# Combining three dilated attention groups: weights per token and head instead of per element, and two slots more for a split operand

## The chip, the cores and the metric

The kernel runs on one core of a Trainium2 chip. The metric is the device time of one execution in microseconds (us). TensorE does the matrix products, VectorE (DVE) and ScalarE (ACT) the elementwise work, GpSimd (POOL) and SyncE (SP) mostly issue transfers; 16 DMA engines move the data.

## The reference

One layer of an encoder over 1024 tokens with 1024 features, all in float32. Three branches of token mixing read the same normalized input: dilated attention (A), retention (R) and attention into a memory (M). Each is projected, gated and added:

```
merged = gate_A*(y_A @ W_pa) + gate_R*(y_R @ W_pr) + gate_M*(y_M @ W_pm)
h = h + merged @ W_out
```

Branch A has three groups of 4 heads of 64, with dilations 1, 4 and 16 (a group with dilation d works on d interleaved subsequences). The change is in how the groups are weighted: a softmax over the groups' log-sum-exp, per token and head.

```
alpha = softmax(stack([lse_0, lse_1, lse_2]), axis=0)     # per head, token
y_A   = stack([o_0, o_1, o_2]) * alpha[..., None]
```

## The kernel before

**Products.** A float32 product is made of three matmuls on rounded operands: each operand is split into a high and a low part (`hilo`: a cast on ScalarE makes `wh` or `yh`, a subtraction on VectorE makes `wl` or `yl`), and `mm3` issues high x high, high x low and low x high. The weights stream from DRAM through SyncE's queue into `wraw` and are split on arrival.

**Dilated attention.** Six pairs of heads, numbered i = 0 to 5 as 3s + g (g the group, s the half of its 4 heads). `attn_dil(i)` loads q, k and v of the pair (`qkv_d`, issued by SyncE), computes scores, and leaves in `U` (128 rows: 2 heads x 64 features; 1024 tokens) the output, stored to `u_d`; and per token and head the negated maximum `nm` and the sum `l`, on 128x16 tiles. Inside a dilated pair the tokens stand in the order of the subsequences; `unperm` puts U back into token order when it leaves PSUM. This stage is merged with the twelve steps of the gates, whose weights are the `wraw<-in_w_gate_dram` of SyncE's queue; TensorE has its matmuls to do there while the pairs' scores go through the other engines.

**Projections.** Then come three projections, one for each branch, in the order R, M, A (`s0`, `s1`, `s2`; b0, b1, b2 are the branches). `proj_steps` does 8 blocks of 128 output features each; a block accumulates over kt = 6, 4 and 6 slabs of y, in PSUM tiles `accg`: 36, 24 and 36 matmuls. The slabs are loaded raw (`yraw`, by SyncE) and split into `yh` and `yl`, which live in a pool of 12 slots (6 slabs): a slab of the next branch gets a slot when the last block of the one before has read its last. `yraw`, `U` and the gates `sg` share a pool of 8 slots of their own (`ab`).

**Combining.** `combine(s)` weighs the three groups of half s, and stores to `ya_d`, from which the third projection reads. Both calls are merged with the first projection. It computes lse = ln(l) - nm on 128x16 tiles; `spread` repeats each value over 64 columns (`lw`), TensorE transposes `lw` into PSUM (`pst`), and ScalarE copies it, put into token order, to a full tile `L` of 128x1024. Then `comb` works on halves of 128x512: maximum, three subtractions, three exponentials, sum, reciprocal, and two multiplications of U per group.

**Order.** The program is written in steps which a scheduler merges into one fixed order for each engine; an engine waits at its next instruction until its inputs and its slot are there. A DMA that waits holds up those behind it on the queue of the same engine.

Of the kernel before, what the change touches and what calls it, by code (L numbers as in the profile page):

```python
# [17 lines left out]
P = 128  # L18
# [130 lines left out]
def encoder_block(ctx: ExitStack, tc: tile.TileContext, x, mem, vec, w_mix, w_gate, w_pa, w_pr, w_pm,  # L149
# [26 lines left out]
    u_d = dram.tile([6 * P, S], F32, name="u_d")  # L176
    sg_d = dram.tile([3 * D, S], F32, name="sg_d")
# [602 lines left out]
    def attn_dil(i, ap_, stats):  # L780
# [7 lines left out]
        def begin():  # L788
            for j, n in ((2, "v"), (0, "q"), (1, "k")):
                st[n] = ab(n)  # L790
                nc.sync.dma_start(st[n], qkv_d[(3 * i + j) * P:(3 * i + j + 1) * P, :])
            loc["V"] = ap_.tile([P, 11, P], F32, name="V", tag="V")
            loc["U"] = ap_.tile([P, S], F32, name="U", tag="U")
            loc["nm"] = st_p.tile([P, 2, 8], F32, name="nm", tag="nm", bufs=6)
            loc["l"] = st_p.tile([P, 2, 8], F32, name="l", tag="l", bufs=6)
# [72 lines left out]
        def tail():  # L868
            stats[i] = (loc["nm"], loc["l"])
            nc.gpsimd.dma_start(u_d[i * P:(i + 1) * P, :], loc["U"])  # L870

# [17 lines left out]

    def combine(s, stats, ap_):  # L890
        loc = {}

        def lse():
            loc["st"] = [stats[3 * s + g] for g in range(3)]
            loc["U"] = [ab("U") for g in range(3)]
            for g in range(3):
                nc.gpsimd.dma_start(loc["U"][g], u_d[(3 * s + g) * P:(3 * s + g + 1) * P, :])
            loc["lse"] = ap_.tile([P, 3, 2, 8], F32, name="lse", tag="lse")
            for g in range(3):
                nc.vector.tensor_copy(loc["lse"][:, g], loc["st"][g][1])  # L900
            nc.scalar.activation(loc["lse"], loc["lse"], AF.Ln)
            for g in range(3):
                nc.vector.tensor_sub(loc["lse"][:, g], loc["lse"][:, g], loc["st"][g][0])
            loc["L"] = []

        def spread(g):
            loc["w"] = []
            for b in range(2):
                W2 = ap_.tile([P, 4, 2, 64], F32, name="lw", tag="sm", bufs=3)
                nc.vector.tensor_copy(W2, loc["lse"][:, g, :, 4 * b:4 * b + 4].rearrange("p h t -> p t h")  # L910
                                      [:, :, :, None].to_broadcast([P, 4, 2, 64]))
                loc["w"].append(W2)

        def bcast(g):
            L = ap_.tile([P, S], F32, name="L", tag="L", bufs=3)
            for b, W2 in enumerate(loc.pop("w")):
# [4 lines left out]
                if DIL[g] == 1:  # L921
                    nc.scalar.copy(L[:, b * HALF:(b + 1) * HALF], ps)
                else:
                    unperm(L, ps, DIL[g], b)
            loc["L"].append(L)

        def comb(h):
            c = slice(h * HALF, (h + 1) * HALF)
            L = [t[:, c] for t in loc["L"]]
            m = ap_.tile([P, HALF], F32, name="cm", tag="sm", bufs=3)  # L930
            z = ap_.tile([P, HALF], F32, name="cz", tag="sm", bufs=3)
            nc.vector.tensor_tensor(m, L[0], L[1], op=ALU.max)
            nc.vector.tensor_tensor(m, m, L[2], op=ALU.max)
            for g in range(3):
                nc.vector.tensor_sub(L[g], L[g], m)
                nc.scalar.activation(L[g], L[g], AF.Exp)
            nc.vector.tensor_add(z, L[0], L[1])
            nc.vector.tensor_add(z, z, L[2])
            for a in range(2):
                nc.vector.reciprocal(z[:, a * 256:(a + 1) * 256], z[:, a * 256:(a + 1) * 256])  # L940
            for g in range(3):
                u = loc["U"][g][:, c]
                k = 2 * g + s
                nc.vector.tensor_mul(u, u, L[g])
                nc.vector.tensor_mul(u, u, z)
                (nc.gpsimd, nc.scalar)[s].dma_start(ya_d[k * P:(k + 1) * P, c], u)

        steps = [lambda g=g, f=f: f(g) for g in range(3) for f in (spread, bcast)]
        return [lse] + steps + [lambda: comb(0), lambda: comb(1)]
# [147 lines left out]
    def y_part(r):  # L1097

        a, b = (y_p.tile([P, S], F32R, name=t, tag="y", bufs=12) for t in ("yh", "yl"))
        hilo(a, b, r)  # L1100
        return a, b
# [110 lines left out]
    def y_load(bi, ks):  # L1212
        for k in ks:
            y_r[bi, k] = y_raw(bi, k)
# [9 lines left out]
    def y_split(bi, kt):  # L1224
        y_load(bi, [k for k in range(kt) if (bi, k) not in y_r])
        y_hl[bi] = list(zip(*[y_part(y_r.pop((bi, k))) for k in range(kt)]))
# [7 lines left out]
    psb.update(pool=psG, bufs={"t": 2})  # L1234
    cb_p = pg.enter_context(pool("cb_p", side="right"))
# [3 lines left out]
    def proj_steps(bi, kt):  # L1239
        def begin():  # L1240
            if bi not in y_hl:
                y_split(bi, kt)
# [28 lines left out]
    run(merge(s0, combine(0, stats, cb_p) + combine(1, stats, cb_p)))  # L1271
    y_load(b1, range(2))
    run(s1[:-2])
# [499 lines left out]
```

## Time and profile before

| | |
|---|---|
| time, median of 3 runs | 1881.91 us (1880.28 to 1887.35) |
| profiled execution: its own time | 1879.56 us |
| its span, first to last instruction | 1877.8 us |
| busy in the span: TensorE, VectorE, ScalarE | 98%, 69%, 50% |

The times of single instructions come from the profiled execution, and count from the start of its span. 1.76 us of its time lie outside the span. A busy share is an average over stages of different kinds, so a stage is read by its own stretch of time.

### The profile page before, as it was taken

How to read it: one execution, taken by the hardware profiler on the slowest of the kernel's cores; microseconds unless marked ns; L12 is line 12 of the kernel's file. 1: busy time of each engine (PE TensorE's matmuls, PEld its weight loads, DVE VectorE, ACT ScalarE, POOL GpSimd, SP SyncE). 2: the span in 40 equal slices, each digit the busy share in tenths (PEclk: the TensorE clock that was granted, in tenths of full speed). 3: DMA queues.
4: the chain of work that ended last, by engine and by line, in shares of the span. 5: the costliest groups of instructions: out<-in, count | busy, mean ns of one | idle time of the engine just before them, and what ended most of it. 6: DMA issues, size and time to landing. Idle time of an engine off the chain costs nothing.

```text
span 1877.8 us, 24304 instructions
## 1 busy us (share of the span) xinstructions
PE 1831.2 (98%) x9254; PEld 1520.4 (81%) x9254; DVE 1290.9 (69%) x2243; ACT 930.9 (50%) x1524; POOL 120.4 (6%) x222
## 2 busy tenths in 40 slices
PE   7999999999999999999998999989999999999997
PEld 6889988888877777777786889967888888888886
DVE  7554464658796555555588654577888787899976
ACT  7354342435686566655633223545454545445444
POOL 1000010110000000000110100000000000020001
PEclk9999999999999999999998999989999999999999
DMA  6211112112233333224546625312232222296543
GB/s 254 90 51 51 46 34 68 68 60 87 79 118 118 113 124 112 77 92 166 192 157 218 210 88 204 104 43 90 68 101 79 90 79 90 91 353 247 176 161 118
DMA packets 65989, 223.70 MB, mean 119 GB/s; under 512 B 7760, under 2 KB 7888, under 8 KB 65744
## 3 DMA queue, kind: packets, MB, share of 16 engines
q1 hardware_dynamic: 41760, 138.77, 21.7%
q0 software_dynamic: 22096, 79.70, 11.2%
q10 hardware_dynamic: 2016, 3.67, 0.5%
q8 instruction: 73, 1.20, 0.3%
q14 instruction: 44, 0.36, 0.1%
HBM read 168.64 MB, written 53.48 MB: 118 GB/s over the span
## 4 chain that ended last, share of the span: by engine, by line
PE 86%; DVE 6%; ACT 5%; issue 2%; DMA 1%; POOL 0%; SPq 0%; POOLq 0%; ACTq 0%; DVEq 0%
PE ps L182 11%; PE ps L183 11%; PE ps L181 11%; PE acc L183 6%; PE acc L181 6%; PE acc L182 6%; PE w L181 5%; PE w L182 4%; PE w L183 4%; PE accg L182 2%; PE accg L183 2%; PE accg L181 2%; PE psu L859 2%; PE pss L815 2%; ACT sw L546 2%
## 5 line engine op out<-in xcount | busy, mean ns | idle before, releaser
L186 ACT CAST wh<-wraw 128x1024 fp32r<-128x1024 f32 (+2 forms) x273 | 261.8, 961 | 308.2 <-PE accg L182 84.4
L187 DVE TENSOR_TENSOR wl<-wraw,wh 128x1024 fp32r<-128x1024 f32 (+2 forms) x273 | 303.5, 1113 | 123.8 <-ACT wh L186 118.9
L181 PE MATMUL acc<-nTh,wh 128*128 128x512 f32 x384 | 152.3, 397 | 0.0
L183 PE MATMUL acc<-nTh,wl 128*128 128x512 f32 x384 | 150.4, 392 | 0.0
L182 PE MATMUL acc<-nTl,wh 128*128 128x512 f32 x384 | 150.1, 391 | 0.0
L181 PE MATMUL ps<-wh,th 128*128 128x512 f32 x308 | 119.8, 389 | 0.0
L182 PE MATMUL ps<-wl,th 128*128 128x512 f32 x308 | 119.8, 389 | 0.0
L183 PE MATMUL ps<-wh,th 128*128 128x512 f32 x308 | 119.8, 389 | 0.0
L181 PE MATMUL w<-nTh,wh 128*128 128x512 f32 x272 | 110.6, 407 | 0.0
L182 PE MATMUL accg<-yl,wh 128*128 128x512 f32 x256 | 101.7, 399 | 8.5 <-DVE yl L187 8.5
L182 PE MATMUL w<-nTl,wh 128*128 128x512 f32 x272 | 106.5, 391 | 0.0
L183 PE MATMUL w<-nTh,wl 128*128 128x512 f32 x272 | 106.4, 391 | 0.0
L181 PE MATMUL accg<-yh,wh 128*128 128x512 f32 x256 | 99.3, 397 | 1.7 <-ACT yh L186 1.7
L183 PE MATMUL accg<-yh,wl 128*128 128x512 f32 x256 | 100.7, 395 | 0.0
L183 PEld LDWEIGHTS acc<-nTh,wl 128*128 128x128 f32 x384 | 72.1, 188 | 14.3
L181 PEld LDWEIGHTS acc<-nTh,wh 128*128 128x128 f32 x384 | 72.2, 188 | 14.2 <-DVE rt L548 0.3
L182 PEld LDWEIGHTS acc<-nTl,wh 128*128 128x128 f32 x384 | 72.2, 188 | 13.4
L181 PE MATMUL pso<-wh,mg 128*128 128x256 f32 x256 | 73.2, 286 | 0.0
L186 ACT CAST th<-g 128x512 fp32r<-128x512 f32 x66 | 40.7, 620 | 64.6 <-PE ps L183 43.2
L183 PE MATMUL pso<-wh,mg 128*128 128x256 f32 x256 | 72.5, 283 | 0.0
L182 PE MATMUL pso<-wl,mg 128*128 128x256 f32 x256 | 72.5, 283 | 0.0
L181 PE MATMUL ps<-b,wh 128*128 128x512 f32 x176 | 68.7, 390 | 0.0
(398 smaller groups left out, 4759.3 us busy)
## 6 DMA issues: line engine op xcount, KB each, us to landing
wraw<-in_w_mlp_dram SPq DMA_DIRECT2D x90, 512.0 KB, 4.1
wraw<-in_w_mix_dram SPq DMA_DIRECT2D x48, 512.0 KB, 3.6
wraw<-in_w_gate_dram SPq DMA_DIRECT2D x24, 512.0 KB, 3.6
sg<-sg_d POOLq DMA_DIRECT2D x24, 512.0 KB, 6.0
g_d<-cv POOLq DMA_DIRECT2D x22, 512.0 KB, 2.9
g<-g_d POOLq DMA_DIRECT2D x22, 512.0 KB, 13.6
wraw<-in_w_out_dram SPq DMA_DIRECT2D x16, 512.0 KB, 3.8
sg_d<-ub POOLq DMA_DIRECT2D x12, 512.0 KB, 2.9
```

Of the source, the lines that this page charges most:

```text
L181: nc.tensor.matmul(o, lh, rh, start=first, stop=False, **kw)
L182: nc.tensor.matmul(o, lh, rl, start=False, stop=False, **kw)
L183: nc.tensor.matmul(o, ll, rh, start=False, stop=last, **kw)
L186: nc.scalar.copy(hi, src)
L187: nc.vector.tensor_sub(lo, src, hi.bitcast(F32))
L546: nc.scalar.copy(sw[q * 32:(q + 1) * 32], ps[o * 32:(o + 1) * 32])
L815: nc.tensor.matmul(ps[:, a * w:(a + 1) * w], st["q"][r, q0:q0 + P], st["k"][r, k0:k0 + w], start=True, stop=True)
L859: nc.tensor.matmul(u[64 * i:64 * i + 64, c], loc["V"][:, vslot[k0 + k * P], 64 * i:64 * i + 64], pt[:, k, a], start=k == 0, stop=k == nk - 1)
```

## The change

The factors are now worked out on the 128x16 tiles, per token and head: w_g = l_g * exp(m - nm_g) / z, with m the least of the three nm and z the sum over the groups. `spread` and the transposes stay, 48 of them; then U is multiplied once by the factor, straight from PSUM. The tiles `L`, `cm`, `cz` of 128x512 and their work fall away, as does ScalarE's copy out of PSUM. For that the statistics of the four dilated pairs (1, 2, 4, 5) must be in token order: `attn_dil` stores them to a DRAM tile `st_d` in one transfer of 128x32 single floats, and `stats_of` loads them back in token order, in four transfers of 128x8 single floats for each pair. All 20 transfers are SyncE's. `ya_d` is stored in 6 whole rows of tiles instead of 12 halves.

Besides, slab 0 of branch M gets two slots of its own (`y2_p`), and is split before the last two blocks of the first projection; these two blocks are merged no longer with the combining but stand ahead of the second projection, and three raw slabs are loaded ahead instead of two.

```diff
@@ -174,6 +174,7 @@
     ym_d = dram.tile([512, S], F32, name="ym_d")
     qkv_d = dram.tile([18 * P, S], F32, name="qkv_d")
     u_d = dram.tile([6 * P, S], F32, name="u_d")
+    st_d = dram.tile([6 * 4, S], F32, name="st_d")
     sg_d = dram.tile([3 * D, S], F32, name="sg_d")
 
     def mm3(o, lh, ll, rh, rl, first, last, skip=False):
@@ -791,8 +792,8 @@
                 nc.sync.dma_start(st[n], qkv_d[(3 * i + j) * P:(3 * i + j + 1) * P, :])
             loc["V"] = ap_.tile([P, 11, P], F32, name="V", tag="V")
             loc["U"] = ap_.tile([P, S], F32, name="U", tag="U")
-            loc["nm"] = st_p.tile([P, 2, 8], F32, name="nm", tag="nm", bufs=6)
-            loc["l"] = st_p.tile([P, 2, 8], F32, name="l", tag="l", bufs=6)
+            loc["st"] = st_p.tile([P, 2, 2, 8], F32, name="st", tag="st", bufs=6)
+            loc["nm"], loc["l"] = loc["st"][:, 0], loc["st"][:, 1]
 
         def vnat(b):
             ps = pst()
@@ -866,8 +867,11 @@
                     unperm(loc["U"], u, dil, b)
 
         def tail():
-            stats[i] = (loc["nm"], loc["l"])
+            stats[i] = loc["st"]
             nc.gpsimd.dma_start(u_d[i * P:(i + 1) * P, :], loc["U"])
+            if dil > 1:
+                nc.sync.dma_start(st_d[4 * i:4 * i + 4, :].rearrange("c (t p) -> p c t", p=P),
+                                  loc["st"].rearrange("p a h t -> p (a h) t"))
 
         def second(t):
             if 0 <= t < 8:
@@ -887,66 +891,59 @@
         o = dst.rearrange("p (l r) -> p r l", r=dil)[:, b * nr:(b + 1) * nr, :]
         nc.scalar.copy(o, u.rearrange("p (r l) -> p r l", r=nr))
 
+    def stats_of(i):
+
+        dil = DIL[pairs[i][0]]
+        if dil > 1:
+            stats[i] = st_p.tile([P, 2, 2, 8], F32, name="sto", tag="sto", bufs=4)
+            for c in range(4):
+                nc.sync.dma_start(stats[i].rearrange("p a h t -> p (a h) t")[:, c],
+                                  st_d[4 * i + c, :].rearrange("(r t l) -> l r t", r=dil, t=8))
+
     def combine(s, stats, ap_):
         loc = {}
...
+        nm, l = ([stats[3 * s + g][:, q] for g in range(3)] for q in range(2))
+
+        def begin():
             loc["U"] = [ab("U") for g in range(3)]
             for g in range(3):
                 nc.gpsimd.dma_start(loc["U"][g], u_d[(3 * s + g) * P:(3 * s + g + 1) * P, :])
...
+            w, m, z = (ap_.tile([P] + sh + [2, 8], F32, name=n, tag=n) for n, sh in
+                       (("cw", [3]), ("cm", []), ("cz", [])))
+            loc["w"] = w
+            nc.vector.tensor_tensor(m, nm[0], nm[1], op=ALU.min)
+            nc.vector.tensor_tensor(m, m, nm[2], op=ALU.min)
             for g in range(3):
...
+                nc.vector.tensor_sub(w[:, g], m, nm[g])
+            nc.scalar.activation(w, w, AF.Exp)
             for g in range(3):
...
+                nc.vector.tensor_mul(w[:, g], w[:, g], l[g])
+            nc.vector.tensor_add(z, w[:, 0], w[:, 1])
+            nc.vector.tensor_add(z, z, w[:, 2])
+            nc.vector.reciprocal(z, z)
+            for g in range(3):
+                nc.vector.tensor_mul(w[:, g], w[:, g], z)
 
         def spread(g):
-            loc["w"] = []
+            loc["lw"] = []
             for b in range(2):
-                W2 = ap_.tile([P, 4, 2, 64], F32, name="lw", tag="sm", bufs=3)
-                nc.vector.tensor_copy(W2, loc["lse"][:, g, :, 4 * b:4 * b + 4].rearrange("p h t -> p t h")
+                W2 = ap_.tile([P, 4, 2, 64], F32, name="lw", tag="lw", bufs=4)
+                nc.vector.tensor_copy(W2, loc["w"][:, g, :, 4 * b:4 * b + 4].rearrange("p h t -> p t h")
                                       [:, :, :, None].to_broadcast([P, 4, 2, 64]))
-                loc["w"].append(W2)
-
...
+                loc["lw"].append(W2)
+
+        def weigh(g):
+            k = 2 * g + s
+            for b, W2 in enumerate(loc.pop("lw")):
                 ps = pst()
                 for a in range(4):
                     nc.tensor.transpose(ps[:, a * P:(a + 1) * P],
                                         W2[:, a].rearrange("p a b -> p (a b)"), ident)
...
+                u = loc["U"][g][:, b * HALF:(b + 1) * HALF]
+                nc.vector.tensor_mul(u, u, ps)
+            (nc.gpsimd, nc.scalar)[s].dma_start(ya_d[k * P:(k + 1) * P, :], loc["U"][g])
+
+        return [begin] + [lambda g=g, f=f: f(g) for g in range(3) for f in (spread, weigh)]
 
 
     def attn_mem(h, qm, cp):
@@ -1094,9 +1091,9 @@
         nc.sync.dma_start(r, y_src[bi][k * P:(k + 1) * P, :])
         return r
 
-    def y_part(r):
-
-        a, b = (y_p.tile([P, S], F32R, name=t, tag="y", bufs=12) for t in ("yh", "yl"))
+    def y_part(r, own=None):
+
+        a, b = ((own or y_p).tile([P, S], F32R, name=t, tag="y", bufs=2 if own else 12) for t in ("yh", "yl"))
         hilo(a, b, r)
         return a, b
 
@@ -1222,8 +1219,13 @@
     y_hl = {}
 
     def y_split(bi, kt):
-        y_load(bi, [k for k in range(kt) if (bi, k) not in y_r])
-        y_hl[bi] = list(zip(*[y_part(y_r.pop((bi, k))) for k in range(kt)]))
+
+        have = y_hl.setdefault(bi, ([], []))
+        ks = range(len(have[0]), kt)
+        y_load(bi, [k for k in ks if (bi, k) not in y_r])
+        for k in ks:
+            for r, t in zip(have, y_part(y_r.pop((bi, k)), y2_p if bi == b1 and k < 1 else None)):
+                r.append(t)
 
     y_split(b0, order[0][2])
     box["late"].pop()()
@@ -1232,14 +1234,14 @@
 
     psG = pg.enter_context(pool("psG", space=PS))
     psb.update(pool=psG, bufs={"t": 2})
+    y2_p = pg.enter_context(pool("y2_p"))
     cb_p = pg.enter_context(pool("cb_p", side="right"))
     mg = [n_p.tile([P, S], F32, name=f"mg{k}", tag="n", bufs=16) for k in range(KT - 1)] + [ab("mg")]
     mgh, mgl = [], []
 
     def proj_steps(bi, kt):
         def begin():
-            if bi not in y_hl:
-                y_split(bi, kt)
+            y_split(bi, kt)
 
         def one(c):
             wh, wl = W.get()
@@ -1268,9 +1270,12 @@
         return [begin] + [lambda c=c: one(c) for c in range(KT)]
 
     s0, s1, s2 = (proj_steps(bi, kt) for bi, _, kt in order)
-    run(merge(s0, combine(0, stats, cb_p) + combine(1, stats, cb_p)))
-    y_load(b1, range(2))
-    run(s1[:-2])
+    for i in range(6):
+        stats_of(i)
+    run(merge(s0[:-2], combine(0, stats, cb_p) + combine(1, stats, cb_p)))
+    y_load(b1, range(3))
+    y_split(b1, 1)
+    run(s0[-2:] + s1[:-2])
     y_load(b2, range(4))
     run(s1[-2:] + s2)
     pg.close()
```

Where instructions now stand is shown at three places, with before first. Lines 791, 1094, 225, 187, 1261 and 1263 of before are lines 792, 1091, 226, 188, 1263 and 1265 of the changed kernel.

**SyncE's queue in the stage of the pairs.** First the rows of before from the gate weights that follow the loads of pair 3 to the loads of pair 5:

```order
L225 DMA wraw<-in_w_gate_dram 128x1024 x4
L791 DMA v<-qkv_d 128x1024
L791 DMA q<-qkv_d 128x1024
L791 DMA k<-qkv_d 128x1024
L225 DMA wraw<-in_w_gate_dram 128x1024 x4
L791 DMA v<-qkv_d 128x1024
L791 DMA q<-qkv_d 128x1024
L791 DMA k<-qkv_d 128x1024
```

Then the same piece of the changed kernel; `st` are the statistics of pair 4, `sto` the same in token order:

```order
L226 DMA wraw<-in_w_gate_dram 128x1024 x4
L792 DMA v<-qkv_d 128x1024
L792 DMA q<-qkv_d 128x1024
L792 DMA k<-qkv_d 128x1024
L226 DMA wraw<-in_w_gate_dram 128x1024 x2
L873 DMA st_d<-st 128x32x1
L900 DMA sto<-st_d 128x8x1 x4
L226 DMA wraw<-in_w_gate_dram 128x1024 x2
L792 DMA v<-qkv_d 128x1024
L792 DMA q<-qkv_d 128x1024
L792 DMA k<-qkv_d 128x1024
```

The store of pair 4's statistics and their four loads now stand between the gate weights, ahead of the loads of pair 5. For pair 2 it is the same (three of its loads, then two gate weights, then v, q and k of pair 3).

**VectorE where the second projection begins.** Before, from the last halves of the combining to the splits of branch M's slabs (`yl`):

```order
L945 TENSOR_TENSOR U<-U,cz 128x512 x3
L933 TENSOR_TENSOR cm<-cm,L 128x512
L187 TENSOR_TENSOR yl<-yraw,yh 128x1024
L935 TENSOR_TENSOR L<-L,cm 128x512 x3
L944 TENSOR_TENSOR U<-U,L 128x512
L937 TENSOR_TENSOR cz<-L 128x512
L944 TENSOR_TENSOR U<-U,L 128x512
L938 TENSOR_TENSOR cz<-cz,L 128x512
L944 TENSOR_TENSOR U<-U,L 128x512
L940 RECIPROCAL cz<-cz 128x256 x2
L187 TENSOR_TENSOR yl<-yraw,yh 128x1024
L945 TENSOR_TENSOR U<-U,cz 128x512 x3
```

Now, from the gate products (`mg`) of the seventh block of the first projection on:

```order
L1263 TENSOR_TENSOR mg_7913<-accg,sg 128x512 x2
L188 TENSOR_TENSOR wl<-wraw,wh 128x512
L188 TENSOR_TENSOR yl<-yraw,yh 128x1024 x2
L1263 TENSOR_TENSOR mg<-accg,sg 128x512 x2
L188 TENSOR_TENSOR wl<-wraw,wh 128x512
L188 TENSOR_TENSOR yl<-yraw,yh 128x1024
L1265 TENSOR_TENSOR sg<-accg,sg 128x512 x2
```

No instruction of the combining is left between the splits.

**VectorE where the first projection begins.** Before:

```order
L1067 TENSOR_TENSOR ub<-ub,w 128x512
L187 TENSOR_TENSOR wl<-wraw,wh 128x768
L187 TENSOR_TENSOR yl<-yraw,yh 128x1024
L1071 TENSOR_TENSOR ua<-ua,w 128x512
L187 TENSOR_TENSOR yl<-yraw,yh 128x1024 x2
L910 COPY lw<-lse 128x512
L187 TENSOR_TENSOR wl<-wraw,wh 128x768
L187 TENSOR_TENSOR yl<-yraw,yh 128x1024
```

Now:

```order
L1064 TENSOR_TENSOR ub<-ub,w 128x512
L188 TENSOR_TENSOR wl<-wraw,wh 128x768
L188 TENSOR_TENSOR yl<-yraw,yh 128x1024
L1068 TENSOR_TENSOR ua<-ua,w 128x512
L915 TENSOR_TENSOR cm<-cm,sto 128x16
L188 TENSOR_TENSOR yl<-yraw,yh 128x1024 x2
L943 TENSOR_TENSOR U<-U,pst 128x512
L188 TENSOR_TENSOR yl<-yraw,yh 128x1024 x3
```

Ahead of the second slab there now stands an instruction that reads the statistics of pair 5 in token order (`sto`), and ahead of the fourth one that reads a loaded `U`.

## Rows read from the trace of the kernel before

**Rows 1.** The page: engines' busy time, and TensorE's granted clock in 40 slices.
```profile
PE 1831.2 (98%) x9254; PEld 1520.4 (81%) x9254; DVE 1290.9 (69%) x2243; ACT 930.9 (50%) x1524; POOL 120.4 (6%) x222
...
PEclk9999999999999999999998999989999999999999
```

**Rows 2.** The waits of TensorE: total us, times, longest.
```profile
PE accg L182 <- DVE yl L187: 8.5, 4, 4.6
```

**Rows 3.** Three stretches, matmuls into `accg` alone: us; busy (instructions).
```profile
923.74:997.60 73.86, 68.05 (x288) 53.20 (x287) 9.32 (x14) 1.00 0.57 196
997.60:1054.90 57.30, 48.29 (x192) 38.56 (x193) 10.77 (x17) 0.91 0.64 224
1054.90:1120.30 65.40, 65.40 (x290) 53.95 (x288) 11.20 (x17) 1.00 0.34 113
```

**Rows 4.** Stretches of 10 us, all instructions (TensorE's clock behind the busy times).
```profile
1000.00:1010.00 10.00, 5.43 (x15) 3.94 (x14) 10.00 (x16) 3.81 (x5) 0.53 (x1) 0.69 0.52 184
1010.00:1020.00 10.00, 6.81 (x22) 4.74 (x21) 8.86 (x9) 1.05 (x1) 1.57 (x3) 0.80 0.42 116
```

**Rows 5.** The first projection's matmuls into `pst` alone.
```profile
923.74:997.60 73.86, 6.40 (x48) 5.58 (x48) 0.00 (x0) 10.01 (x12) 1.00 0.57 196
```

**Rows 6.** The timeline of TensorE at the start of the second projection.
```profile
1005.07 0.79 PE L182 MATMUL accg<-yl,wh 128*128 128x512 f32 x1 [4.57 <-DVE yl L187]
...
1014.24 0.80 PE L182 MATMUL accg<-yl,wh 128*128 128x512 f32 x1 [3.19 <-DVE yl L187]
```

**Rows 7.** The timeline of VectorE there.
```profile
1009.74 3.37 DVE L940 RECIPROCAL cz<-cz 128x256 f32<-128x256 f32 x2
1013.01 1.17 DVE L187 TENSOR_TENSOR yl<-yraw,yh 128x1024 fp32r<-128x1024 f32 x1
```

**Rows 8.** Groups on VectorE from 905 to 1020 us: count, busy us, mean ns.
```profile
L940 DVE RECIPROCAL cz<-cz 128x256 f32<-128x256 f32 x8 | 13.6, 1731 | 0.0
...
L944 DVE TENSOR_TENSOR U<-U,L 128x512 f32<-128x512 f32 x12 | 8.3, 689 | 0.0
...
L910 DVE COPY lw<-lse 128x512 f32<-128x512 f32 x12 | 4.6, 420 | 0.0
...
L903 DVE TENSOR_TENSOR lse<-lse,nm 128x16 f32<-128x16 f32 x6 | 0.7, 170 | 1.5 <-ACT lse L901 1.5
```

**Rows 9.** Groups on ScalarE from 905 to 1020 us.
```profile
L888 ACT COPY L<-pst 128x512 f32<-128x512 f32 x8 | 7.9, 1091 | 1.1 <-ACT L L922 1.0
```

**Rows 10.** The timeline of SyncE's queue: start, us of issuing, transfer.
```profile
22.56 0.46 SPq L484 DMA_DIRECT2D zeta<-in_t_zeta_dram  x1
...
734.81 0.37 SPq L791 DMA_DIRECT2D v<-qkv_d  x1
...
857.03 1.58 SPq L791 DMA_DIRECT2D v<-qkv_d  x1
```

**Rows 11.** The timeline of ScalarE: the last statistics of pairs 2 and 4.
```profile
729.04 0.19 ACT L826 ACTIVATION_READ_ACCUMULATOR sm<-sm,nm 128x1 f32 x1
...
848.67 0.19 ACT L826 ACTIVATION_READ_ACCUMULATOR sm<-sm,nm 128x1 f32 x1
```

**Rows 12.** The timeline of TensorE: first use of v of pairs 3 and 5.
```profile
744.60 0.60 PE L801 MATMUL pst<-ident,v 128*128 128x128 f32 x4
...
865.41 0.60 PE L801 MATMUL pst<-ident,v 128*128 128x128 f32 x4
```

**Rows 13.** DMA issues from 734 to 745 us: count, KB, median us to landing.
```profile
v<-qkv_d SPq DMA_DIRECT2D x1, 512.0 KB, 6.7
```

**Rows 14.** DMA issues from 857 to 868 us.
```profile
v<-qkv_d SPq DMA_DIRECT2D x1, 512.0 KB, 6.9
```

**Rows 15.** DMA issues of the whole run.
```profile
out_dram<-hr SPq DMA_DIRECT2D x8, 256.0 KB, 2.1
...
zeta<-in_t_zeta_dram SPq DMA_DIRECT2D x1, 6.0 KB, 8.1
```

**Rows 16.** The timeline of VectorE at the start of the first projection.
```profile
926.25 1.23 DVE L187 TENSOR_TENSOR yl<-yraw,yh 128x1024 fp32r<-128x1024 f32 x1 [1.09 <-ACT yh L186]
```

More of the change, by code (lines that the diff above doesn't have):

```diff
@@ L888, in unperm @@
         nc.scalar.copy(o, u.rearrange("p (r l) -> p r l", r=nr))
+    def stats_of(i):
[5 more added lines that the diff above has]
+                                  st_d[4 * i + c, :].rearrange("(r t l) -> l r t", r=dil, t=8))
     def combine(s, stats, ap_):
         loc = {}
-        def lse():
-            loc["st"] = [stats[3 * s + g] for g in range(3)]
+        nm, l = ([stats[3 * s + g][:, q] for g in range(3)] for q in range(2))
+        def begin():
             loc["U"] = [ab("U") for g in range(3)]
@@ L897, in lse @@
                 nc.gpsimd.dma_start(loc["U"][g], u_d[(3 * s + g) * P:(3 * s + g + 1) * P, :])
-            loc["lse"] = ap_.tile([P, 3, 2, 8], F32, name="lse", tag="lse")
+            w, m, z = (ap_.tile([P] + sh + [2, 8], F32, name=n, tag=n) for n, sh in
[3 more added lines that the diff above has]
+            nc.vector.tensor_tensor(m, m, nm[2], op=ALU.min)
             for g in range(3):
-                nc.vector.tensor_copy(loc["lse"][:, g], loc["st"][g][1])
-            nc.scalar.activation(loc["lse"], loc["lse"], AF.Ln)
+                nc.vector.tensor_sub(w[:, g], m, nm[g])
+            nc.scalar.activation(w, w, AF.Exp)
             for g in range(3):
-                nc.vector.tensor_sub(loc["lse"][:, g], loc["lse"][:, g], loc["st"][g][0])
-            loc["L"] = []
+                nc.vector.tensor_mul(w[:, g], w[:, g], l[g])
[4 more added lines that the diff above has]
+                nc.vector.tensor_mul(w[:, g], w[:, g], z)
         def spread(g):
-            loc["w"] = []
+            loc["lw"] = []
             for b in range(2):
-                W2 = ap_.tile([P, 4, 2, 64], F32, name="lw", tag="sm", bufs=3)
-                nc.vector.tensor_copy(W2, loc["lse"][:, g, :, 4 * b:4 * b + 4].rearrange("p h t -> p t h")
+                W2 = ap_.tile([P, 4, 2, 64], F32, name="lw", tag="lw", bufs=4)
+                nc.vector.tensor_copy(W2, loc["w"][:, g, :, 4 * b:4 * b + 4].rearrange("p h t -> p t h")
                                       [:, :, :, None].to_broadcast([P, 4, 2, 64]))
-                loc["w"].append(W2)
-        def bcast(g):
-            L = ap_.tile([P, S], F32, name="L", tag="L", bufs=3)
-            for b, W2 in enumerate(loc.pop("w")):
+                loc["lw"].append(W2)
+        def weigh(g):
+            k = 2 * g + s
+            for b, W2 in enumerate(loc.pop("lw")):
                 ps = pst()
@@ L920, in bcast @@
                                         W2[:, a].rearrange("p a b -> p (a b)"), ident)
[L921 to L949, printed above, removed]
+                u = loc["U"][g][:, b * HALF:(b + 1) * HALF]
+                nc.vector.tensor_mul(u, u, ps)
+            (nc.gpsimd, nc.scalar)[s].dma_start(ya_d[k * P:(k + 1) * P, :], loc["U"][g])
+        return [begin] + [lambda g=g, f=f: f(g) for g in range(3) for f in (spread, weigh)]
     def attn_mem(h, qm, cp):
```

## The prediction, written before the change was timed

> **What bounds the kernel now.** I read the page first: TensorE is busy 98% of the span, and its granted clock is at nine tenths or more in all 40 slices but one, at eight tenths [rows 1]. So the change can pay only where TensorE stands still or runs at the lower clock. The waits of TensorE over the whole run name such a place: 8.5 us, in four pieces, in which a matmul into `accg` waits for a `yl` of VectorE [rows 2]. Then I cut the projections into stretches and looked at the matmuls into `accg` alone [rows 3]. The third projection (A) takes 65.40 us and is busy all of it; it has 288 matmuls by the code, so one costs 65.40/288 = 0.227 us. The second (M) has 192, worth 43.6 us, and takes 57.30: 13.7 us too many. Of these 57.30 - 48.29 = 9.0 are idle, and 4.7 are matmuls that ran longer. The stretches of 10 us show when: from 1000 to 1010 TensorE is busy 5.43 us at a granted clock of 0.69 on average, from 1010 to 1020 6.81 us at 0.80 [rows 4]. Its two levels are 2.4 and 1.2 GHz, and it fell to the lower one after TensorE had stood still for `yl`. The first projection (R) takes 73.86 us [rows 3], where 65.4 for `accg` and 6.40 for its 48 transposes [rows 5] make 71.8: 2.1 too many.
>
> What is late is read from two timelines at the beginning of the second projection. TensorE waits 4.57 us until 1005.07 and 3.19 us until 1014.24, each time for `yl` [rows 6]. VectorE begins the second of these `yl` at 1013.01, straight behind two reciprocals of the combining that take 3.37 us [rows 7], and from 1000 to 1010 it is busy all 10 us [rows 4]. In the order of before a `yl` stands behind ten operations of the combining. So the combining is not short of cover on average, but its end lies past the end of the first projection, and the splits of the next operand queue behind it.
>
> **What the change removes.** On VectorE: eight reciprocals, 13.6 us; the 36 multiplications and subtractions of lines 935, 944 and 945, of 0.69 us like those of line 944, and 16 operations of lines 932 to 938 of the same shape, together 52 x 0.69 = 36 us [rows 8]. On ScalarE the copies of `L` (7.9 us for the eight that permute [rows 9]) and twelve exponentials. What is added on VectorE: 14 operations on 128x16 for each half, priced by line 903 at 0.17, 28 x 0.17 = 4.8 us, and 12 multiplications of 0.69 = 8.3; the 12 `lw` of 0.42 stay [rows 8]. VectorE does 13.6 + 36 - 4.8 - 8.3 = 36 us less. None of that counts by itself. What counts is that the splits of branch M's slabs are no longer behind it.
>
> *The beginning of the second projection.* Slab 0 is split early into slots of its own, so TensorE has work while the last block of the first projection releases slabs 0 to 2 for the next splits; no operation of the combining stands between these splits in the new order. What can still be late is the last slab: its raw load stands on SyncE behind weights whose slot comes free only near the end of the seventh block, and a load of 512 KB takes 6.7 us as v of pair 3 shows [rows 13]. Followed by hand through the new order it is split 1 to 2 us before TensorE asks for it. Bounds: nothing left of the 13.7, or one wait left of the size of the smaller of before, 3.2 [rows 6]. I take 0.5 left: 13.7 - 0.5 = **13.2 us gained**.
>
> *The rest of the first projection.* Of its 2.1 us too many about half are at its start, where `yl` waits 1.09 us for `yh` [rows 16], which the change leaves. The other half, waits behind the combining, I let go: **1.0 gained**, bounds 0 and 2.1. At the start two instructions are new ahead of splits: one needs the statistics of pair 5, one a loaded `U`, and each may hold the split behind it. Their loads land at about the time at which VectorE gets there. Bounds 0 and 3 us; I take **0.5 lost**.
>
> **What the change adds on SyncE's queue.** Twenty transfers of single floats, four stores of 4096 pieces and sixteen loads of 1024. The first load of a pair must wait until the store has landed, and SyncE stands there, with weights and v, q, k behind it. Call T the time from the start of the store to its landing, I the time that issuing a load takes. Pair 2's last statistics are read at 729.04 + 0.19 = 729.23, pair 4's at 848.86 [rows 11]. For pair 3, three loads and two weights follow, the weights at 0.37 each like v, and then v, which was issued at 734.81 before [rows 10]: it is late by 729.23 + T + 3I + 0.74 - 734.81 = T + 3I - 4.84. Its slack is 744.60 (first use [rows 12]) - 734.81 - 6.7 (landing [rows 13]) = 3.09, so TensorE stands still for T + 3I - 7.93. For pair 5, issued at 857.03 [rows 10], four loads precede: late by T + 4I - 7.43; slack 865.41 [rows 12] - 857.03 - 6.9 [rows 14] = 1.48; still for T + 4I - 8.91. Together **2T + 7I - 16.8**, where both are positive. (The store of pair 1 delays v of pair 2 little, which is used long after; that of pair 5 is the start of the first projection above.)
>
> The trace of before has no transfer of single floats. From below: I is 0.37, as for any 128 rows [rows 10], and T = 0.37 + 2.1, as a store of 256 KB lands [rows 15]; then nothing stands still. From above: issuing costs per piece what it costs per row, 4096/128 x 0.37 = 11.8 for the store and 3.0 for a load, T = 11.8 + 2.1 = 13.9: pair 3 stands 15.0 us, pair 5 17.0, together 32. The nearest row is `zeta`, 128 pieces of 48 bytes: issued in 0.46 [rows 10], landed in 8.1 [rows 15], though behind large loads. I take T = 8 and I = 0.46, because a load of small pieces there took no longer to issue than one of large ones: 16 + 3.2 - 16.8 = **2.4 lost** (1.45 and 0.93).
>
> The Trainium skill (DMA: Bandwidth & Descriptors, Rules for kernel authors) speaks against this edit: an access whose last dimension is strided lowers to one descriptor per element, and should be rearranged. Its section Bandwidth gives about 10.5 ns a packet; for 256 pieces on each of 16 engines that is an estimated 2.7 us, T about 5, and the sum would be 2.4 us better. No run here shows it yet.
>
> **The sum**: -13.2 - 1.0 + 0.5 + 2.4 = -11.3 us. On the profiled execution's own 1879.56, which is 2.35 below the median shown but inside the runs' 1880.28 to 1887.35 to within 0.72, that is **1868.3 us**.
>
> **Rivals.**
> *SyncE's queue is held by the single floats*, the slower one. It is the term 2T + 7I - 16.8 with large T or I. For it speaks that nothing in the profile prices 4096 pieces in one transfer; against it `zeta`'s 0.46 us. The rest of the sum is -13.7, so it decides from 2T + 7I = 30.5 on, with I = 0.46 at T = 13.7. At the upper bound 1879.56 - 13.7 + 32 = 1898; at the middle of both ranges (T = 8.2, I = 1.7) 16.4 + 11.9 - 16.8 = 11.5, which is 1877. The rule of the Trainium skill cited above is of this kind, since it counts descriptors.
> *The wait moves to the raw loads.* Slabs 1 to 3 of branch M still need slots of `ab` and of the split pool at the end of the first projection. If the last one comes as late as the smaller wait of before, 3.2 us, and the clock falls after it as it did (4.7 for two waits, 2.4 for one), 5.6 of the 13.7 stay: 1879.56 - 11.3 + 5.1 = 1873. The order speaks against it, with no combining between the splits.
> *The combining was covered anyway*, so that nothing changes: 1879 to 1882. Against it stand the four waits for `yl`, which end right behind its operations.
>
> **How the numbers follow.** One measurement of this kernel can tell about 0.5%, 9.4 us, from no change. Forecast, 1863.5 to 1870.2 (from no stall and all of both terms, -15.8, to just 9.4 gained): 0.60. Single floats that take back most, 1870 to 1889: 0.17. The wait moved to the raw loads, or a gain that went elsewhere, 1872 to 1880: 0.10. SyncE held, above 1889: 0.13. So faster 0.60, same 0.27, slower 0.13. The range holds 8 in 10: from 1863 up to 1881, which leaves out the slower case and the upper part of the second; the likeliest case's own is 1863.5 to 1870.2.
>
> **What would show it.** In the profile after: no wait of `accg` for `yl` of more than 1 us, the second projection in 44 to 45 us at full clock; VectorE with some 18 us of combining. On SyncE the first load of `sto` about 8 us behind the store of its pair, and v of pairs 3 and 5 issued 1 to 5 us later than before. The prediction is wrong if issuing one of these transfers takes several us, if TensorE waits for `V` or `sto` by more than 5 us in all, or if the second projection still begins with idle time.

## The result, and the profile after

The changed kernel takes 1907.29 us (median of 4 runs, 1904.06 to 1909.79) against 1881.66 of before: 1.0138 times, 95% interval 1.0124 to 1.0152. It is 26 us slower, where 11 us less were forecast. The span of its profiled execution is 1904.3 us, 26.5 more.

The waits of TensorE over the whole run answer to [rows 2]:

```profile
PE pst L802 <- DMA v<-qkv_d: 25.5, 3, 13.6
...
PE accg L182 <- ACT yh L187: 8.1, 1, 8.1
```

The first was not there before; of the second kind, a wait for `yh`, there were 1.7 us, 1.4 of them in the second projection and none ahead of the first. The waits for `yl` in the second projection are gone, as the stretches of the three projections show, with the matmuls into `accg` alone (us, then busy time and number of each engine; the last three columns are TensorE's clock, the DMA share and GB/s); they answer to [rows 3]:

```profile
962.60:1037.20 74.60, 68.73 (x286) 54.07 (x287) 9.45 (x14) 0.97 0.75 261
1037.20:1080.80 43.60, 43.60 (x195) 36.08 (x193) 10.92 (x17) 1.00 0.61 210
1080.80:1146.70 65.90, 65.89 (x291) 54.24 (x289) 11.60 (x17) 1.00 0.32 106
```

The second projection is busy all its 43.6 us. From the first matmul into `accg` on, the three take 1146.7 - 962.6 = 184.1 us, where before they took 1120.3 - 923.7 = 196.6: 12.5 gained. But the first of these matmuls comes at 962.6 instead of 923.7, 38.9 us later. The two numbers make the 26.4 of the result. Of the 38.9 us, 25.5 and 8.1 are the two waits above; 5.3 are left.

What they wait behind stands on SyncE's queue; each row is the issue of a transfer, with its start and how long issuing took. It answers to [rows 10]:

```profile
678.23 0.39 SPq L873 DMA_DIRECT2D st_d<-st  x1
678.78 7.58 SPq L792 DMA_DIRECT2D v<-qkv_d  x1
...
731.37 0.38 SPq L873 DMA_DIRECT2D st_d<-st  x1
749.46 3.63 SPq L900 DMA_DIRECT2D sto<-st_d  x3
753.19 1.87 SPq L226 DMA_DIRECT2D wraw<-in_w_gate_dram  x2
755.16 0.37 SPq L792 DMA_DIRECT2D v<-qkv_d  x1
...
867.06 0.38 SPq L873 DMA_DIRECT2D st_d<-st  x1
883.63 3.02 SPq L900 DMA_DIRECT2D sto<-st_d  x4
...
933.53 0.38 SPq L873 DMA_DIRECT2D st_d<-st  x1
950.72 0.63 SPq L900 DMA_DIRECT2D sto<-st_d  x1
951.46 2.30 SPq L1091 DMA_DIRECT2D yraw<-yr_d  x3
```

Issuing a store of 4096 single floats takes 0.38 us. But from there to the first load, which waits for its landing, 18.1, 16.6 and 17.2 us pass (for pairs 2, 4 and 5; for pair 1 it is 15.6). SyncE also stands ahead of each store, until the pair's statistics are there, 74.1 us for the four, and holds up what is queued behind:

```profile
SPq L873 <- ACT sm L827: 74.1, 4, 28.1
```

The v of pair 3 is then issued at 755.16, 20 us later than before. TensorE waits for v of pair 2, a little, and for v of pairs 3 and 5:

```profile
696.80 0.63 PE L802 MATMUL pst<-ident,v 128*128 128x128 f32 x4 [1.76 <-DMA v<-qkv_d]
...
760.50 1.09 PE L802 MATMUL pst<-ident,v 128*128 128x128 f32 x4 [13.63 <-DMA v<-qkv_d]
...
762.23 0.63 PE L184 MATMUL w<-nTh,wl 128*128 128x512 f32 x1
762.66 0.63 PE L182 MATMUL w<-nTh,wh 128*128 128x512 f32 x1
...
893.83 1.09 PE L802 MATMUL pst<-ident,v 128*128 128x128 f32 x4 [10.10 <-DMA v<-qkv_d]
```

After the wait for pair 3 a matmul starts every 0.43 us (762.23 to 762.66) instead of every 0.23: the lower level of the clock, as before in the second projection. In stretches of 2 us the granted clock is 0.50 from 762 to 764 and from 894 to 898, and full again from 766 and 900 on. An estimate from these rows: TensorE works some 9 us at the lower level behind the two long waits and loses half of them, so that 4 to 5 of the 5.3 us that are not waits are the clock's.

### The profile page after: what moved, and what is told of

Its sections match the earlier page's. It is cut to its first block, busy times and chain, and to the rows that moved or that the text cites. A ratio compares the mean times of both kernels' runs of the same rounds, so it can differ in the third digit from the quotient of the medians.

```text
span 1904.3 us, 24234 instructions
## 1 busy us (share of the span) xinstructions
PE 1831.9 (96%) x9254; PEld 1521.2 (80%) x9254; DVE 1257.9 (66%) x2211; ACT 913.4 (48%) x1499; POOL 118.8 (6%) x219
## 4 chain that ended last, share of the span: by engine, by line
PE 84%; ACT 5%; DMA 5%; DVE 4%; issue 1%; SPq 1%; POOL 0%; POOLq 0%; ACTq 0%; DVEq 0%
PE ps L183 11%; PE ps L184 10%; PE ps L182 10%; PE acc L184 5%; PE acc L182 5%; PE acc L183 5%; PE w L182 4%; PE w L184 4%; PE w L183 4%; PE accg L183 3%; PE accg L184 3%; PE accg L182 3%; PE pss L816 2%; ACT sw L547 2%; DMA st_d<-st 2%; PE psu L860 2%
## 6 DMA issues: line engine op xcount, KB each, us to landing
g<-g_d POOLq DMA_DIRECT2D x22, 512.0 KB, 13.6
```

## The experiments

Theory Q, formed from these rows: SyncE stands behind each store, with v, q, k and the slabs of y queued. Its rival C: part of the loss is in the new combining or in the new order. All ratios are to the kernel before, run on the same chip.

**1. Without the transfers.** The store in `tail` and the loads in `stats_of` are left out; the factors are then worked out from the statistics in the order in which they stand, which is not the tokens' order.

```diff
-            if dil > 1:
-                nc.sync.dma_start(st_d[4 * i:4 * i + 4, :].rearrange("c (t p) -> p c t", p=P),
-                                  loc["st"].rearrange("p a h t -> p (a h) t"))
...
```

> The changed kernel without the 20 transfers of statistics: the factors are worked out from the statistics as they stand, so the tokens of the dilated pairs get each other's weights; the work on the engines is the same. Theory Q (SyncE stands 16 to 18 us behind each store until it has landed, and v, q, k and the slabs are queued behind it): the waits of 13.6, 10.1 and 8.1 us go, the gain of the second projection stays, 1866 to 1870 us. Rival C (part of the loss is in the new combining or in the new order of the projections): above 1876, with a wait of several us at the first projection's start left.

Measured: 1865.01 us, 0.9923 (0.9909 to 0.9937). No wait for v, and at the projections only small ones:

```profile
PE accg L183 <- DVE yl L188: 1.3, 3, 0.6
PE accg L182 <- ACT yh L187: 0.2, 1, 0.2
```

All of the loss goes with the transfers; the rest of the change is worth 14.6 us (1879.59 - 1865.01).

**2. Without the transfers and without the slots.** Slab 0 gets slots of the common pool again, and the steps stand as before.

```diff
-            for r, t in zip(have, y_part(y_r.pop((bi, k)), y2_p if bi == b1 and k < 1 else None)):
+            for r, t in zip(have, y_part(y_r.pop((bi, k)), None)):
...
-run(merge(s0[:-2], combine(0, stats, cb_p) + combine(1, stats, cb_p)))
-y_load(b1, range(3))
-y_split(b1, 1)
-run(s0[-2:] + s1[:-2])
+run(merge(s0, combine(0, stats, cb_p) + combine(1, stats, cb_p)))
+y_load(b1, range(2))
+run(s1[:-2])
```

> As the run without transfers, and without the two slots of its own for slab 0 of branch M, the split of it ahead and the last two blocks' place behind the combining (that part is as before). If the shorter combining alone makes the gain: within 2 us of the run without transfers. If the slots carry part of it: 3 to 6 us more, since TensorE then waits at the start of the second projection for a slot, a cast (1.04) and a subtraction (1.22).

Measured: 1871.27 us, 0.9958 (0.9944 to 0.9972), 6.3 more than without transfers alone. The second projection begins with a wait again:

```profile
999.71 0.73 PE L182 MATMUL accg<-yh,wh 128*128 128x512 f32 x2 [2.54 <-ACT yh L187]
```

So of the 14.6 us the shorter combining gives 8.3, and the slots and the order of the steps, put on top of it, 6.3. What these would give with the old combining was not tried.

**3. The transfers alone**, in the kernel before, with `nm` and `l` in one tile `st` as in the change.

```diff
...
+            if dil > 1:
+                nc.sync.dma_start(st_d[4 * i:4 * i + 4, :].rearrange("c (t p) -> p c t", p=P),
+                                  loc["st"].rearrange("p a h t -> p (a h) t"))
+    for i in range(6):
+        stats_of(i)      # loads sto; nobody reads it
```

> The kernel before with the 20 transfers alone added (nobody reads what they load). Theory Q: the same three waits as in the changed kernel, some 32 us and the lower clock after them: 1910 to 1922. Rival C (the loss needs the new combining): below 1890.

Measured: 1922.67 us, 1.0229 (1.0213 to 1.0245), 0.7 above the range expected, with the waits of the changed kernel and those of before together:

```profile
PE pst L802 <- DMA v<-qkv_d: 26.6, 3, 14.1
...
PE accg L182 <- ACT yh L187: 9.1, 2, 7.7
PE accg L183 <- DVE yl L188: 8.7, 3, 4.6
```

Rival C falls: the transfers cost some 43 us with the old combining and the old order of the projections, and 42 with the new ones.

**4. The statistics transposed before the store.**

```diff
+ps = pst()
+nc.tensor.transpose(ps[:32, :P], loc["st"].rearrange("p a h t -> p (a h t)"), ident)
+sT = ap_.tile([P, 1, 2, P], F32, name="sT", tag="pt_s", bufs=2)[:32, 0, 0]
+nc.vector.tensor_copy(sT, ps[:32, :P])
-nc.sync.dma_start(st_d[4 * i:4 * i + 4, :].rearrange("c (t p) -> p c t", p=P),
-                  loc["st"].rearrange("p a h t -> p (a h) t"))
+nc.sync.dma_start(st_d[4 * i:4 * i + 4, :].rearrange("c (t p) -> (c t) p", p=P), sT)
```

> The changed kernel with the statistics of a pair transposed on TensorE (one transpose of 128x32, one copy on VectorE) and stored as 32 rows of 512 bytes instead of 4096 single floats; the 16 loads of 1024 single floats stay as they are. Theory Q with the pieces of the store as the cause: it lands in 2 to 4 us, the waits for v shrink to 0 to 4 us in all, 1867 to 1873. Rival L (the loads of single floats hold the queue as well, 0.6 to 2 us each): 1875 to 1888.

Measured: 1866.84 us, 0.9931 (0.9918 to 0.9944): 0.7% faster than the kernel before, and 40 us faster than the changed one. From the DMA issues (count, KB, median us to landing) the stores, 32 rows of 512 bytes each, and the loads of single floats, as they were:

```profile
sto<-st_d SPq DMA_DIRECT2D x16, 4.0 KB, 4.5
...
st_d<-sT SPq DMA_DIRECT2D x4, 16.0 KB, 2.8
```

With all 16 loads left in, only 1.8 us are missing to the run without transfers, too little to tell from noise. But the edit moved more than the pieces of the store. In the new order of SyncE's queue the store of pair 2 stands behind v, q and k of pair 3, and the first three slabs stand ahead of pair 5's store; in the changed kernel it is the other way round in both places:

```profile
735.53 0.33 SPq L792 DMA_DIRECT2D v<-qkv_d  x1
...
743.15 0.32 SPq L877 DMA_DIRECT2D st_d<-sT  x1
...
884.30 2.20 SPq L1094 DMA_DIRECT2D yraw<-yr_d  x3
...
915.99 0.69 SPq L877 DMA_DIRECT2D st_d<-sT  x1
```

So run 4 shows a remedy, and not which part of it helps: the fast store or its later place. The loads too no longer stand ahead of v, so that rival L is not settled by it. A slow store in the later place was not tried. Run 10 holds the order and changes the store.

**5. A price list in the kernel**: run 1 with a store of another form for each pair, and nobody waiting for it.

```diff
+f = loc["st"].rearrange("p a h t -> p (a h) t")
+if i == 0:
+    nc.sync.dma_start(sa_d.rearrange("c (t p) -> p c t", p=P), f)
+elif i == 1:
+    nc.sync.dma_start(sb_d.rearrange("c (t p) -> p c t", p=P), f[:, :2])
...
+elif i == 4:
+    nc.sync.dma_start(se_d.rearrange("c (p t) -> p c t", p=P), f)
```

> The run without transfers, with one store of statistics for each pair to a DRAM tile that nobody reads, so that no queue waits for it: pair 0 as in the change, 4096 single floats; pair 1 2048; pair 2 1024; pair 3 128 pieces of 128 bytes; pair 4 512 pieces of 32 bytes; pair 5 2048 single floats that are scattered on the SBUF side alone and lie side by side in DRAM. Theory P (the landing goes by the number of pieces, 16.4 us/256 = 64 ns for each piece of an engine): 16, 9, 5, 2 to 3, 4 to 5, 9 us. Rival D (single floats scattered in DRAM are what is slow, not the pieces): the last 3 to 5 us. Time by theory Q, since nobody waits: 1863 to 1868; above 1872 if the pieces themselves slow the other transfers down.

Measured: 1870.18 us, 0.9946 (0.9931 to 0.9961). The landings, for pairs 0 to 5: 16.2, 11.9, 12.4, 1.4, 1.8 and 16.4 us. Neither theory P nor rival D fits: 1024 floats take no less than 2048, and floats side by side in DRAM are as slow as scattered ones. And these stores, for which nobody waits, seem to cost some 4 us (0.9946 against 0.9923 without transfers; the two intervals overlap a little); TensorE waits 4.1 us at the first projection's start, where run 1 has only small waits. From 903 to 916 us the slabs land late beside the last store (6.4 us was the median of before):

```profile
yraw<-yr_d SPq DMA_DIRECT2D x3, 512.0 KB, 16.3
...
sf_d<-st SPq DMA_DIRECT2D x1, 8.0 KB, 16.4
```

**6 and 7. Another queue.** First only the loads (run 6), then the stores too (run 7), go to GpSimd's queue.

```diff
-nc.sync.dma_start(stats[i].rearrange("p a h t -> p (a h) t")[:, c],        # 6 and 7
+nc.gpsimd.dma_start(stats[i].rearrange("p a h t -> p (a h) t")[:, c],
...
-nc.sync.dma_start(st_d[4 * i:4 * i + 4, :].rearrange("c (t p) -> p c t", p=P),    # 7
+nc.gpsimd.dma_start(st_d[4 * i:4 * i + 4, :].rearrange("c (t p) -> p c t", p=P),
```

> The changed kernel with the 16 loads of statistics on GpSimd's queue; the stores of single floats stay on SyncE's, and land as late as before. Theory Q: SyncE waits for nothing, TensorE no longer for v (0 to 3 us in all); GpSimd stands behind the stores instead, with stores of gates and of U queued there, and pair 5's statistics come at the same time after its store, some 20 us: 1866 to 1880. Rival D' (the traffic of single floats is what costs): 1895 or more.

> The changed kernel with both the stores and the loads of statistics on GpSimd's queue. Theory Q: as with the loads there, 1866 to 1880, unless GpSimd's issuing of 4096 pieces takes long of itself (then its later stores and the loads of U and of the gates are late, and the first projection waits): up to 1900.

Measured: 1901.12 us, 1.0117 (1.0100 to 1.0134), and 1899.52 us, 1.0102 (1.0087 to 1.0117). Here theory Q falls as it stood, and rival D' (1895 or more: the traffic itself costs) fits the time. In run 7 SyncE waits for no store, v of pair 3 is issued at 736.03, 1.2 us later than before, and still TensorE waits for it. The DMA issues of its stretch from 734 to 751 us, against 6.7 of [rows 13]:

```profile
wraw<-in_w_gate_dram SPq DMA_DIRECT2D x2, 512.0 KB, 16.0
v<-qkv_d SPq DMA_DIRECT2D x1, 512.0 KB, 16.9
```

In its stretch beside the third store the last column, what the DMA engines moved in GB/s, is 29; at about the same place without transfers (run 1, second fence) it is 195:

```profile
861.00:875.00 14.00, 14.00 (x71) 11.10 (x70) 4.47 (x5) 6.30 (x9) 0.00 (x0) 1.00 0.55 29
```

```profile
855.00:870.00 15.00, 15.00 (x73) 12.12 (x74) 3.89 (x6) 6.21 (x9) 0.53 (x1) 1.00 0.57 195
```

So such a store holds up not only the queue that waits for it: what is issued beside it, from either queue, lands about when it does. Theory Q' takes Q's place: the store holds the transfers, and SyncE's waiting adds its own delay (13.6 us of waiting for v of pair 3 in the changed kernel, 7.1 in run 7).

The waits for v are only 13.9 us of run 7's loss. As large is what happens at the first projection: GpSimd waits for pair 5's store before it loads its statistics, VectorE stands at the instruction that reads them (`cm<-sto`, ahead of the second slab's split), and TensorE behind that split (in run 6: 18.3 and 10.7 us):

```profile
DVE cm L915 <- DMA sto<-st_d: 15.1, 1, 15.1
...
PE accg L183 <- DVE yl L188: 12.3, 1, 12.3
```

**8. The price alone**, behind the last transfer of the kernel before. The helper that makes one pair of transfers, shortened:

```diff
+d = dram.tile([rows, cols], F32, name=n)
+nc.sync.dma_start(store(d), hx[:, at])     # hx: 32 columns of the last result tile
+nc.sync.dma_start(hx[:, :m], load(d))      # ten such pairs, each behind the one ahead
```

> The kernel before, with ten pairs of transfers behind its last one, each waiting for the one ahead, while nothing else moves: a store of a piece of the result tile to a DRAM tile, and a load of it back. Stores: pa 128 pieces of 128 bytes; pb, pc, pd 4096, 2048, 1024 single floats scattered over DRAM; pe 2048 pieces of 8 bytes; pf 1024 of 16; pg 512 of 32; ph 2048 single floats side by side in DRAM. The loads are of rows, but those of pi and pj, of 4096 and 1024 single floats. Theory P (time goes by the number of pieces, whatever their size): pb 16, pc and pe 9, pd and pf 5, pg 4 us, and the load of pi 16. Theory S (it goes by single floats, and 8 bytes and more are fast): pe, pf, pg 2 us. Theory N (alone each is fast, and the 16 us came from other transfers beside it): pb below 6 us. If a store counts and a load does not: the load of pi below 6.

Measured, one run; the names are explained in the expectation, the last number is the landing in us:

```profile
pb<-hr SPq DMA_DIRECT2D x1, 16.0 KB, 15.8
...
pc<-hr SPq DMA_DIRECT2D x1, 8.0 KB, 11.0
...
pd<-hr SPq DMA_DIRECT2D x1, 4.0 KB, 10.5
...
pe<-hr SPq DMA_DIRECT2D x1, 16.0 KB, 7.4
...
pf<-hr SPq DMA_DIRECT2D x1, 16.0 KB, 3.2
...
pg<-hr SPq DMA_DIRECT2D x1, 16.0 KB, 1.8
...
ph<-hr SPq DMA_DIRECT2D x1, 8.0 KB, 11.0
...
hr<-pi SPq DMA_DIRECT2D x1, 16.0 KB, 4.2
```

Theory N falls: 4096 floats take 15.8 us with nothing beside them. So does P: 1024 floats (pd) take three times as long as 1024 pieces of 16 bytes (pf). Theory S, by which 8 bytes and more are fast, misses pe and pf. And a load of 4096 single floats takes 4.2 us. What fits is how many pieces go into one stretch of 512 bytes of DRAM: 128 in pb, pc, pd and ph, 64 in pe, 32 in pf, 16 in pg. (Their sizes differ in the same steps; run 9 tells these apart.)

**9. The floats spread.**

```diff
+nc.sync.dma_start(d.rearrange("(t p) x -> p t x", p=P)[:, :, 0], hx[:, 0:n])   # distance: 4 x bytes
```

> As the price list behind the last transfer, all stores of single floats, each followed by a load of 128 floats back: qa 128 floats side by side in 512 bytes of DRAM; qb and qc 1024 and 4096, each float in a stretch of 512 bytes of its own; qd, qe, qf, qg, qh 1024 at distances of 256, 128, 64, 32 and 8 bytes; qi 1024 side by side, 8 of a partition next to each other; qj 128, each in 512 bytes of its own. Theory R (writes into the same stretch of 512 bytes wait for each other, some 0.08 to 0.1 us each: 128, 64, 32, 16 pieces a stretch took 10.5 to 15.8, 7.4, 3.2, 1.8 us in the list before): qa 8 to 12, qb 2 to 3, qc 2 to 5, qd 2, qe 2, qf 2, qg 2 to 3, qh 6 to 8, qi 10.5, qj 1.5. Theory P' (a single float has its price wherever it goes, about 10 us for 1024): qa and qj 1.5 to 3, all of 1024 about 10.

Measured, one run:

```profile
qa<-hr SPq DMA_DIRECT2D x1, 0.5 KB, 7.6
...
qb<-hr SPq DMA_DIRECT2D x1, 4.0 KB, 2.4
...
qc<-hr SPq DMA_DIRECT2D x1, 16.0 KB, 7.4
...
qg<-hr SPq DMA_DIRECT2D x1, 4.0 KB, 3.1
...
qh<-hr SPq DMA_DIRECT2D x1, 4.0 KB, 4.4
...
qi<-hr SPq DMA_DIRECT2D x1, 4.0 KB, 8.2
...
qj<-hr SPq DMA_DIRECT2D x1, 0.5 KB, 1.4
```

(Lines of loads between them are left out; qd, qe and qf took 2.4, 2.7 and 2.7.) Theory P' falls: 128 floats side by side take 7.6 us, the same number 512 bytes apart 1.4, and 1024 spread ones 2.4 instead of 10.5. (qa stands first, behind the stores of the result. The first store of run 8, pa, took 2.5 us, where the same form later took 1.4; so some of the 7.6 may be that.) Theory R holds in its direction; in size it missed qc (7.4, not 2 to 5), so the number of pieces counts too, qh (4.4, not 6 to 8), qi (8.2, not 10.5) and qa, somewhat below its 8 to 12. That the stretch is 512 bytes long is not shown: 1024 floats are down to 4.4 us at a distance of 8 bytes and to 3.1 at 32, where 64 and 16 of them still share such a stretch, and gain little beyond. A shorter stretch would fit as well.

**10. The same in the kernel.**

```diff
-st_d = dram.tile([6 * 4, S], F32, name="st_d")
+st_d = dram.tile([6 * 4, S, P], F32, name="st_d")     # element 0 of each 512 bytes is used
...
```

> The changed kernel with one thing altered: the statistics in DRAM stand 512 bytes apart instead of side by side, so that each float of a store has a stretch of its own; the same 4 stores of 4096 and 16 loads of 1024 single floats, the same order on SyncE's queue. Theory R (floats side by side in one stretch wait for each other): a store lands in 7 to 8 us as alone, the waits for v shrink from 23.7 to 3 us or less, the first projection starts without the wait of 8.1: 1866 to 1873. Theory P' (single floats are slow wherever they go) or the count of transfers as the cause: above 1895.

Measured: 1878.34 us (1872.23 to 1883.45, 11 runs), 0.9986 (0.9975 to 0.9996). The store lands in 8.2 us, and the waits shrink:

```profile
PE pst L802 <- DMA v<-qkv_d: 7.1, 2, 3.7
```

With the same transfers in the same order, 29 of the 42 us that lie between the changed kernel and the run without transfers are back (1907.3 - 1878.3 of 1907.3 - 1865.0). This is the run that shows the store's landing as a cause, and the larger part of the loss. What is left, some 13 us, is the 8.2 us of landing, the loads that still stand ahead of v, and the place of the store in the order; no run tells these apart. The time is 5 us above the range expected, in part because 7.1 us of waiting for v were left and not 3. The transposed store, with its other order, is better by 11.5.

## Why the prediction was wrong

*The gain* was right. The end of the combining kept the splits of the second projection waiting; without it that projection runs without a gap. The terms "13.2 gained", "1.0 gained" and the 0.5 of the new instructions' cost make 13.7 from the first projection's begin on; the three projections gained 12.5 in the changed kernel, where the first had waits of its own, and in run 1, which is faster by 14.6 as a whole, they take 182.5 us, 14.1 less. That the slots carry much of this was in the reasoning and not in the numbers: run 2 puts it, with the order of the steps, at 6.3. (Two small slips change nothing: [rows 1] has two slices at eight tenths and not one, the second of them behind the projections; and 1879.56 - 15.8 is 1863.8, not 1863.5.)

*The formula* for the two stalls was right too. For pair 3, T + 3I - 7.93 with the measured T = 18.1 and 3I = 3.6 gives 13.8; TensorE waited 13.63. For pair 5, T + 4I - 8.91 with 16.6 and 3.0 gives 10.7; it waited 10.1. That it fits to 0.2 us for pair 3 is partly luck: the two weights took 1.87 us on the queue and not 0.74, and v was there 5.3 us after its issue and not 6.7.

*The step that failed* is the size of T: "I take T = 8", within bounds of 2.5 and 13.9. It measured 15.6 to 18.1, above both. The two stalls came to 23.7 us where 2.4 were forecast; 2T is 34.7 and not 16, and 7I is 6.7 and not 3.2, since issuing a load took 0.75 to 1.2 us where 0.46 was taken. The upper bound put the price of the pieces into issuing, 11.8 us, and left the landing at 2.1; issuing took 0.38 and all the time was in the landing. The row that I took T from, `zeta`, is a load, of pieces of 48 bytes. Run 8 shows why it says nothing: a load of 4096 single floats lands in 4.2 us, a store in 15.8. The trace had no row from which the store could be bounded from above, and the prediction should have said so in place of a bound. The rival that decides "at T = 13.7" with I = 0.46 is the one that came true; it was given 0.13, and its upper end of 1898 was still too low.

*What was not seen* is that the store holds other transfers. My formula has SyncE's wait alone. In the changed kernel this makes no difference for v of pairs 3 and 5, which are issued after the landing; it is part of what defeated the obvious remedy, another queue (runs 6 and 7). It shows at the v of pair 2, which follows pair 1's store: its issue took 7.58 us instead of 0.37, and TensorE waited 1.76 us for it. The prediction let this wait go, because that v "is used long after". It also had no term for the lower clock behind a stall, the 4 to 5 us estimated above.

*The start of the first projection* was a term of 0.5 with an upper bound of 3. In the kernel before, the first slabs were issued in good time:

```profile
883.40 1.33 SPq L1094 DMA_DIRECT2D yraw<-yr_d  x3
```

In the changed kernel they were issued only at 951.46, behind pair 5's store, and TensorE waited 8.1. The prediction had this store delay a small instruction on VectorE, and not the slabs behind it on SyncE's queue. The small instruction did wait too, 3.2 us, and a matmul 1.6 us behind it; in runs 6 and 7, where the slabs came sooner, it cost TensorE 10.7 and 12.3.

*The rule of the Trainium skill* (DMA: Bandwidth & Descriptors, Rules for kernel authors), to rearrange an access whose last dimension is strided, agrees with the landings: 2.8 us for the store of rows in run 4, 16 to 18 for that of single floats. The Trainium skill's figure of about 10.5 ns a packet (DMA: Bandwidth & Descriptors, Bandwidth) is given there for loads that GpSimd issues, and did not carry over to this store: the estimate of T that I worked out from it was 5, the store took 16 to 18.

The other two rivals are settled: the wait did not move to the raw loads of branch M (43.6 us of 43.6 busy), and the combining was not covered (run 2 gains 8.3 us by it alone).

## What to carry to other kernels

Before an edit moves a small tile to DRAM, look at the pieces in which it is written: a store of 4096 floats side by side, each a piece of its own, took 15.8 us where the same bytes in 128 pieces of 128 bytes took 1.4 (runs 8 and 5), and the transfers beside it landed late. A transpose of 128x32 on TensorE and one copy make rows of it, and the load can do the reordering: a load of as many single floats took 4.2 us. Look also at where such a store stands on its queue, since the queue waits at it, first for what it stores and then for its landing: in run 4 a new place in the order went with the fast store. And when the trace has no row for an operation, a bound taken from its nearest neighbour must be of the same direction and the same piece, or it is no bound.

## What was not expected of the hardware

- A store of 4096 single floats side by side lands in 15.8 us alone, 2048 in 11.0, 1024 in 10.5, and 128 in 7.6; 128 floats that are 512 bytes apart land in 1.4, 1024 such in 2.4. Pieces of 8, 16 and 32 bytes take 7.4, 3.2 and 1.8 for the same 16 KB. The Trainium skill (DMA: Bandwidth & Descriptors, Specifications) says that below 512 bytes the DMA engine reads, modifies and writes; that writes into the same stretch wait for each other would fit this and the rows, but it is argued and not shown, and so is the stretch's length.
- While such a store is under way, transfers of 512 KB landed in 16 to 17 us instead of 6 to 7, with the store on SyncE's queue (16.3, run 5) as on GpSimd's (16.9, run 7).
- A load of 4096 single floats landed in 4.2 us (run 8).
